# Even and odd tokens of the split activations stored in two halves and read alternately by the matmuls

## The chip, the core and the metric

The kernel runs on one core of one Trainium2 chip. The metric is the device time in microseconds (us) of one execution, as the median of several runs; lower is better. Five units of the core appear below: TensorE (PE for its matmuls, PEld for loading the stationary operand), VectorE (DVE), ScalarE (ACT), GpSimd (POOL) and SyncE (SP, which here only starts transfers).

## What is computed

Two layers of a decoder trunk on 256 tokens with 16 learned meta tokens ahead of them (272 in all), model width 2048, hidden width 8192, all in float32:

```python
h = concat(meta, x)                                       # 272 tokens x 2048
h = h + gla_mixer(rmsnorm(h), w_in, ..., w_out)           # layer 0: gated linear attention
h = h + (relu(rmsnorm(h) @ w_up) ** 2) @ w_down           # layer 0: MLP
k_sh, v_sh = split(rmsnorm(h) @ w_kv)                     # shared keys and values
h = h + swa_mixer(rmsnorm(h), k_sh, v_sh, w_q, sinks, w_out)   # layer 1: windowed attention
h = h + (relu(rmsnorm(h) @ w_up) ** 2) @ w_down           # layer 1: MLP
return rmsnorm(h[16:])
```

Nearly all of the arithmetic is in the projections: activations of 272 tokens (256 in layer 1, where the meta tokens are needed no more) times weight matrices that are read from HBM once.

## The kernel before

The stream `h` stays in SBUF transposed: 16 tiles of 128 features (partitions) by 272 tokens. A projection is cut into output tiles of 128 features. For each one, `product` fetches two halves of 128x1024 weights (SP starts the transfer), splits each into a rounded part and a rest, and lets TensorE add up 16 steps of 128 input features in one PSUM bank. The weights are the stationary operand (128x128), the activations the moving one, one column for each token.

Every float32 operand is held as two float32r numbers, `hi` (rounded) and `lo` (the rest), and a product is `hi*hi + hi*lo + lo*hi`. For weights `split_weight` makes the two (a ScalarE copy on L89, a VectorE subtraction on L91). For activations the class `Split` (L94) wraps one tile of `2n` columns, `hi` in columns 0 to n and `lo` in columns n to 2n. Such tiles are made in five places:

- `split_x` (L152 to L155): ScalarE scales a stream tile into `x.hi` (L154), VectorE makes `x.lo` (L155); 80 times, for each projection that reads the stream.
- the gated outputs `y` of the linear attention (L691, L692): 16 times.
- the hidden tiles `hid` of the MLP (L720, L721): 128 times.
- the attention outputs `O`, one tile of 16 x 2 x 256 columns that is written from PSUM in pieces: eight of 2 x 240 tokens (L884, L885) and two small ones for the last 16 tokens of each head.

The matmuls that read them are in `passes` (L101). With n = 256 it is "wide": one matmul streams `hi` and `lo` together, 512 columns, into the two halves of a PSUM bank (L109), and a second one adds the weights' rest times `hi`, 256 columns (L110). With n = 272 (layer 0), or where `apart` is false (the query projection, the first round of the attention's output projection, the last product), three matmuls go to one place (L112, L113, L114). The first stage, in which the stream arrives in pieces, issues the same three kinds of matmul by hand (`passes_of` on L273, `block` on L280 and L282, and `rank` on L267).

```python
nc.tensor.matmul(ps[:, :2 * n], wh, x.both, start=begin, stop=False)       # L109
nc.tensor.matmul(ps[:, n:2 * n], wl, x.hi, start=False, stop=end)          # L110
```

The order of TensorE's work is fixed: in the first stage and in the windowed attention by hand-written schedules, elsewhere by the order of the program, which a planner lays out by its own estimate of times. ScalarE and VectorE split weights ahead of TensorE (three buffers each of `hi` and `lo`, four of raw weights), and between these they finish the products.

Of the kernel before, what the change touches and what calls it, by code (L numbers as in the profile page):

```python
# [12 lines left out]
F32R = mybir.dt.float32r  # L13
# [6 lines left out]
P = 128  # L20
D = 2048
KT = D // P
HK = KT // 2
NM = 16
SEQ = 256
L = NM + SEQ
# [19 lines left out]
GRP = QH // KVH  # L46
# [18 lines left out]
def trunk(ctx: ExitStack, tc: tile.TileContext, a: dict, out: bass.AP):  # L65
    nc = tc.nc
# [19 lines left out]
    def split_weight(raw):  # L86
# [4 lines left out]
        nc.vector.tensor_sub(lo, raw, hi.bitcast(F32))  # L91
        return hi, lo

    class Split:  # L94


        def __init__(self, tile_, n):
            self.n, self.both = n, tile_[:, :2 * n]
            self.hi, self.lo = self.both[:, :n], self.both[:, n:]

    def passes(ps, hi, lo, xs, first, last, m=P, apart=True):  # L101

        n = xs[0].n
        wide = apart and 2 * n <= 512
        for k, x in enumerate(xs):
            wh, wl = hi[:, k * m:(k + 1) * m], lo[:, k * m:(k + 1) * m]
            begin, end = first and k == 0, last and k == len(xs) - 1
            if wide:
                nc.tensor.matmul(ps[:, :2 * n], wh, x.both, start=begin, stop=False)  # L109
                nc.tensor.matmul(ps[:, n:2 * n], wl, x.hi, start=False, stop=end)  # L110
            else:
                nc.tensor.matmul(ps[:, :n], wh, x.hi, start=begin, stop=False)  # L112
                nc.tensor.matmul(ps[:, :n], wh, x.lo, start=False, stop=False)  # L113
                nc.tensor.matmul(ps[:, :n], wl, x.hi, start=False, stop=end)  # L114

    def product(src, xs, raws=None, halves=(0, 1), after=None, apart=True, begun=None, pool=acc):

# [33 lines left out]

    def split_x(src, scale_col):  # L152
        x = Split(xp.tile([P, 2 * L], F32R, tag="x", name="x"), src.shape[-1])
        nc.scalar.activation(x.hi, src, AF.Copy, scale=scale_col)  # L154
        nc.vector.scalar_tensor_tensor(x.lo, src, scale_col, x.hi.bitcast(F32), ALU.mult, ALU.subtract)  # L155
        return x
# [59 lines left out]
    with ExitStack() as gla:  # L216
# [35 lines left out]
        wrs = bp.tile([P, KT, RG * 32], F32R, tag="Q", name="wrs")  # L252
        nc.gpsimd.memset(wrs.bitcast(F32), 0.0)
        groups = wrs.rearrange("p k (g r) -> p k g r", r=32)
        xs, sq = [], Square()
        ps_r = aux.tile([P, 512], F32, tag="aux", name="ps_r")
# [5 lines left out]
        def rank(k0, k1):  # L262

            for k in range(k0, k1):
                parts = [(RG * 32, xs[k].hi), ((RG - 1) * 32, xs[k].lo)]
                for i, (m, part) in enumerate(parts if k < KT - 1 else parts[::-1]):
                    nc.tensor.matmul(ps_r[:m, :L], wrs[:, k, :m], part, start=k + i == 0, stop=k + i == KT)  # L267

        first = [(acc if m < 4 else aux).tile([P, 512], F32, tag="acc" if m < 4 else "aux", name="ps") for m in range(NF)]

        def passes_of(m, k, t, w, j):

            nc.tensor.matmul(first[m][:, :L], w[t // 2][:, j * P:(j + 1) * P], xs[k].lo if t == 1 else xs[k].hi, start=k + t == 0, stop=False)  # L273

        def block(m, k0, k1, w):

            for part in range(2):
                for k in range(k0, k1):
                    wk = w[part][:, (k - k0) * P:(k - k0 + 1) * P]
                    nc.tensor.matmul(first[m][:, :L], wk, xs[k].hi, start=False, stop=part == 1 and k == KT - 1)  # L280
                    if part == 0:
                        nc.tensor.matmul(first[m][:, :L], wk, xs[k].lo, start=False, stop=False)  # L282

        def room():
            return [wp.tile([P, HK * P], F32R, tag=t, name=t) for t in ("hi", "lo")]
# [28 lines left out]
        with tc.manual_schedule(engines={mybir.EngineType.PE, mybir.EngineType.Activation, mybir.EngineType.DVE}):  # L314
# [3 lines left out]
            for u in range(2):  # L318
                for m in range(NF):
                    if m == u == 0:  # L320
                        take(0, 1)
                    if m % 2 == 0:
                        w = room()
                    part = m % 2
# [12 lines left out]
            for i, raw in enumerate(pairs):  # L337
                w = room()
                m0, m1 = max(2 * i - 1, 0), 2 * i + 1
# [7 lines left out]
            w = second(0)  # L347
# [4 lines left out]
            w = second(1)  # L352
# [3 lines left out]
            w = second(2)  # L356
# [3 lines left out]
            w = second(3)  # L360
# [27 lines left out]
        with tc.issue_after(scaled_keys.ins):  # L388
            for m in range(NF, 8):
                ps, = product(a["w_in"][8 + m], xs, begun=w5 if m == NF else None, pool=aux if m == NF else acc)  # L390
# [22 lines left out]
        for m in range(8):  # L413
            log_gate(m)
            ps, = product(a["w_in"][m], xs)
# [260 lines left out]
        for m in range(KT):  # L676
            g, mm = divmod(m, 4)
            if mm == 0:
                mix(g)
            ps, = product(a["w_in"][32 + m], xs)  # L680
            gt = tp.tile([P, L], F32, tag="t1", bufs=4, name="gt")
            nc.vector.tensor_mul(gt, ps, rs)
            sg = tp.tile([P, L], F32, tag="t2", bufs=4, name="sg")
            nc.gpsimd.tensor_scalar_max(sg, gt, -80.0)
            nc.scalar.activation(sg, sg, AF.Exp, scale=-1.0)
            nc.scalar.activation(sg, sg, AF.Ln, bias=1.0)
            nc.scalar.activation(sg, sg, AF.Exp, scale=-1.0)
            nc.vector.tensor_mul(gt, gt, sg)
            nc.vector.scalar_tensor_tensor(gt, OT[g][:, mm], no[:, mm:mm + 1], gt, ALU.mult, ALU.mult)
            y = Split(yp.tile([P, 2 * L], F32R, tag="y", bufs=KT, name="y"), L)  # L690
            nc.scalar.copy(y.hi, gt)  # L691
            nc.vector.tensor_sub(y.lo, gt, y.hi.bitcast(F32))  # L692
            ys.append(y)
# [11 lines left out]
    def mlp(layer, xs, sq, cols, finish):  # L705
        n = cols.stop - cols.start
        rs = sq.rstd(D, "rs", split=True)
        with tc.tile_pool(name="hid", bufs=KT) as hp, tc.tile_pool(name="wp2", bufs=1) as wp2:
            for b in range(NB):
                hs = []  # L710
                for m in range(KT):
                    if b == 0 and m == 4:
                        pools.append(wp2)
                    ps = total(product(a[f"w_up{layer}"][b * KT + m], xs))
                    u = tp.tile([P, L], F32, tag="t1", bufs=4, name="u")[:, :n]
                    nc.vector.scalar_tensor_tensor(u, ps, 0.0, rs, ALU.max, ALU.mult)
                    u2 = tp.tile([P, L], F32, tag="t2", bufs=4, name="u2")[:, :n]
                    nc.scalar.square(u2, u)
                    y = Split(hp.tile([P, 2 * L], F32R, tag="hid", name="hid"), n)
                    nc.scalar.copy(y.hi, u2)  # L720
                    nc.vector.tensor_sub(y.lo, u2, y.hi.bitcast(F32))  # L721
                    hs.append(y)
                for m in range(KT):
                    ending = layer == 1 and b == NB - 1 and m == KT - 1
                    for term in product(a[f"w_down{layer}"][b * KT + m], hs, apart=not ending):
                        nc.vector.tensor_add(h[m][:, cols], h[m][:, cols], term)
                    if b == NB - 1:
                        finish(m)
            pools.remove(wp2)
# [12 lines left out]
    with ExitStack() as swa:  # L742
# [62 lines left out]
                nc.scalar.copy(VT[i][:n, g], pt[:n, i * P:(i + 1) * P])  # L805


        O = ap.tile([P, KT, 2, SEQ], F32R, name="O")
        N1, N3 = P - NM, NM
        N2 = N1 + P  # L810

# [24 lines left out]
        class Step:  # L836
# [39 lines left out]
            def values(self):  # L876
                PT, m0 = self.PT, self.m0
                ps = acc.tile([P, 512], F32, tag="acc", name="ps_pv")
                pv = ps[:, :2 * N2].rearrange("p (i q) -> p i q", i=2)
                for t, q, begin, end in ((0, slice(0, N1), True, True), (1, slice(N1, N2), True, False), (2, slice(N1, N2), False, True)):  # L880
                    for par, kv in enumerate(HALVES):
                        nc.tensor.matmul(pv[kv, :, q], VT[t // 2][:, self.pair, kv], PT[t][:, 2 * par:2 * par + 2, :q.stop - q.start], start=begin, stop=end)  # L882
                oh, ol = O[:, m0:m0 + 2, 0, :N2], O[:, m0:m0 + 2, 1, :N2]
                nc.scalar.copy(oh, pv)  # L884
                nc.vector.tensor_sub(ol, pv, oh.bitcast(F32))  # L885

# [22 lines left out]
            def last_values(self):  # L909
                ps = aux.tile([P, 512], F32, tag="aux", name="ps_pv3")  # L910
                for b, nb in enumerate((P, P, NM)):
                    for t, kv in zip(self.PT3, HALVES):
                        nc.tensor.matmul(ps[kv, :P], VT[b][:nb, self.pair, kv], t[:nb, b], start=(b == 0), stop=(b == 2))
                ms = slice(self.pair * GRP, (self.pair + 1) * GRP)
                src = ps[:, :P].rearrange("p (i q) -> p i q", q=N3)
                oh, ol = O[:, ms, 0, N2:], O[:, ms, 1, N2:]
                nc.scalar.copy(oh, src)
                nc.vector.tensor_sub(ol, src, oh.bitcast(F32))

# [7 lines left out]
        with tc.manual_schedule(engines={mybir.EngineType.PE}):  # L927
            steps = []
            for t in range(2 * GRP // 2):
# [23 lines left out]
                for i in range(2):  # L953
# [3 lines left out]
            late = {3: [a4.values, partial(a6.scores, 0), partial(a6.scores, 1)], 5: [a5.transposes],  # L957
                    7: [a5.values, partial(a7.scores, 0), partial(a7.scores, 1)], 8: [a7.last_scores, a6.transposes],
                    10: [a6.values], 11: [a7.transposes], 12: [a7.last_transposes], 13: [a7.values, a7.last_values]}
            ys = [Split(O[:, m].rearrange("p a n -> p (a n)"), SEQ) for m in range(KT)]  # L960
            residual(a["w_out_b"], ys, X, to_mlp, rounds=2, between=late)

    fin = ctx.enter_context(tc.tile_pool(name="fin", bufs=1))
# [95 lines left out]
```

## Time and profile before

| | |
|---|---|
| median of 3 runs | 2179.11 us (2179.04 to 2180.6) |
| span of the profiled execution, first to last instruction | 2177.8 us |
| PE busy / PEld busy | 2163.8 us (99%) / 2055.6 us (94%) |
| DVE / ACT / POOL busy | 1367.1 us (63%) / 1079.2 us (50%) / 194.9 us (9%) |
| moved by the DMA engines | 383.85 MB, 176 GB/s on the mean |
| mean granted TensorE clock | 0.998 |

The profile holds the span alone; the time of the same execution around it isn't given, and the median stands 1.3 us above the span. [...]

### The profile page before, as it was taken

How to read it: one execution, taken by the hardware profiler on the slowest of the kernel's cores; microseconds unless marked ns; L12 is line 12 of the kernel's file. 1: busy time of each engine (PE TensorE's matmuls, PEld its weight loads, DVE VectorE, ACT ScalarE, POOL GpSimd, SP SyncE). 2: the span in 40 equal slices, each digit the busy share in tenths (PEclk: the TensorE clock that was granted, in tenths of full speed). 3: DMA queues.
4: the chain of work that ended last, by engine and by line, in shares of the span. 5: the costliest groups of instructions: out<-in, count | busy, mean ns of one | idle time of the engine just before them, and what ended most of it. 6: DMA issues, size and time to landing. Idle time of an engine off the chain costs nothing.

```text
span 2177.8 us, 39097 instructions
## 1 busy us (share of the span) xinstructions
PE 2163.8 (99%) x15978; PEld 2055.6 (94%) x15978; DVE 1367.1 (63%) x1999; ACT 1079.2 (50%) x1729; POOL 194.9 (9%) x209
## 2 busy tenths in 40 slices
PE   9999999999999999999999999999999999999997
PEld 9999999999999999999999999988888888888886
DVE  7799667655455445545556767686656656666665
ACT  6556664444344334433444578755435535544543
POOL 0000123300000000000013111060000000000022
PEclk9999999999999999999999999999999999999999
DMA  7544445555555555555554654465555555555552
GB/s 234 178 153 139 144 148 184 178 210 175 175 174 175 176 176 176 176 174 177 176 175 136 196 167 150 135 229 187 191 187 192 187 191 187 191 187 190 190 187 97
DMA packets 109124, 383.85 MB, mean 176 GB/s; under 512 B 13328, under 2 KB 15888, under 8 KB 108944
## 3 DMA queue, kind: packets, MB, share of 16 engines
q1 hardware_dynamic: 106640, 378.29, 51.7%
q0 software_dynamic: 1152, 2.38, 0.4%
q8 instruction: 125, 2.05, 0.4%
q10 hardware_dynamic: 1152, 0.68, 0.1%
q14 instruction: 55, 0.45, 0.1%
HBM read 376.82 MB, written 2.10 MB: 174 GB/s over the span
## 4 chain that ended last, share of the span: by engine, by line
PE 99%; DMA 0%; DVE 0%; SPq 0%; ACT 0%; issue 0%; DVEq 0%
PE ps L109 23%; PE ps L112 20%; PE ps L114 20%; PE ps L113 20%; PE ps L110 12%; PE ps L280 1%; PE s L860 1%; PE ps_pv L882 1%; PE pt L871 0%; PE ps L282 0%; PE ps_o L667 0%; DMA h<-in_h 0%; PE ps_l L542 0%; DVE scaled L979 0%; PE ps_r L267 0%; DMA raw<-in_w_in 0%
## 5 line engine op out<-in xcount | busy, mean ns | idle before, releaser
L91 DVE TENSOR_TENSOR lo<-raw,hi 128x1024 fp32r<-128x1024 f32 x707 | 872.6, 1235 | 577.7 <-ACT hi L89 570.6
L89 ACT CAST hi<-raw 128x1024 fp32r<-128x1024 f32 x707 | 741.1, 1049 | 991.8 <-PE ps L113 546.5
L112 PE MATMUL ps<-x,hi 128*128 128x272 f32 (+1 forms) x2032 | 585.8, 288 | 0.0
L114 PE MATMUL ps<-x,lo 128*128 128x272 f32 (+1 forms) x2032 | 585.0, 288 | 0.0
L113 PE MATMUL ps<-x,hi 128*128 128x272 f32 (+1 forms) x2032 | 584.5, 288 | 0.0
L113 PEld LDWEIGHTS ps<-x,hi 128*128 128x128 f32 x2032 | 386.0, 190 | 0.3 <-DVE x L155 0.2
L112 PEld LDWEIGHTS ps<-x,hi 128*128 128x128 f32 x2032 | 382.5, 188 | 2.5 <-issue 2.3
L114 PEld LDWEIGHTS ps<-x,lo 128*128 128x128 f32 x2032 | 381.6, 188 | 0.3
L109 PE MATMUL ps<-x,hi 128*128 128x512 f32 x1024 | 357.0, 392 | 0.0
L109 PE MATMUL ps<-hid,hi 128*128 128x512 f32 x1008 | 351.0, 392 | 0.0
L114 PE MATMUL ps<-hid,lo 128*128 128x272 f32 (+1 forms) x1040 | 299.9, 288 | 0.0
L112 PE MATMUL ps<-hid,hi 128*128 128x272 f32 (+1 forms) x1040 | 299.9, 288 | 0.0
L113 PE MATMUL ps<-hid,hi 128*128 128x272 f32 (+1 forms) x1040 | 299.4, 288 | 0.0
L110 PE MATMUL ps<-x,lo 128*128 128x256 f32 x1024 | 287.7, 281 | 0.0
L110 PE MATMUL ps<-hid,lo 128*128 128x256 f32 x1008 | 282.6, 281 | 0.0
L109 PEld LDWEIGHTS ps<-x,hi 128*128 128x128 f32 x1024 | 192.0, 188 | 42.9
L109 PEld LDWEIGHTS ps<-hid,hi 128*128 128x128 f32 x1008 | 188.8, 188 | 41.9
L113 PEld LDWEIGHTS ps<-hid,hi 128*128 128x128 f32 x1040 | 197.8, 190 | 0.0
L112 PEld LDWEIGHTS ps<-hid,hi 128*128 128x128 f32 x1040 | 195.4, 188 | 0.0
L114 PEld LDWEIGHTS ps<-hid,lo 128*128 128x128 f32 x1040 | 195.4, 188 | 0.0
L110 PEld LDWEIGHTS ps<-x,lo 128*128 128x128 f32 x1024 | 193.2, 189 | 0.0
L110 PEld LDWEIGHTS ps<-hid,lo 128*128 128x128 f32 x1008 | 190.2, 189 | 0.3
(259 smaller groups left out, 2102.6 us busy)
## 6 DMA issues: line engine op xcount, KB each, us to landing
raw<-in_w_up SPq DMA_DIRECT2D x256, 512.0 KB, 3.3
raw<-in_w_down SPq DMA_DIRECT2D x256, 512.0 KB, 3.3
raw<-in_w_in SPq DMA_DIRECT2D x91, 512.0 KB, 3.3
raw<-in_w_out_a SPq DMA_DIRECT2D x32, 512.0 KB, 3.3
raw<-in_w_q SPq DMA_DIRECT2D x32, 512.0 KB, 3.5
raw<-in_w_out_b SPq DMA_DIRECT2D x32, 512.0 KB, 3.3
raw<-in_w_kv SPq DMA_DIRECT2D x8, 512.0 KB, 3.4
sw<-qt POOLq DMA_DIRECT2D x32, 64.0 KB, 3.8
```

What stands on the lines that cost most here:

```text
L89: nc.scalar.copy(hi, raw)
L91: nc.vector.tensor_sub(lo, raw, hi.bitcast(F32))
L109: nc.tensor.matmul(ps[:, :2 * n], wh, x.both, start=begin, stop=False)
L110: nc.tensor.matmul(ps[:, n:2 * n], wl, x.hi, start=False, stop=end)
L112: nc.tensor.matmul(ps[:, :n], wh, x.hi, start=begin, stop=False)
L113: nc.tensor.matmul(ps[:, :n], wh, x.lo, start=False, stop=False)
L114: nc.tensor.matmul(ps[:, :n], wl, x.hi, start=False, stop=end)
L280: nc.tensor.matmul(first[m][:, :L], wk, xs[k].hi, start=False, stop=part == 1 and k == KT - 1)
L860: nc.tensor.matmul(s[:, i * n:(i + 1) * n], self.QR[pp, i, o:o + P], KR[pp, self.pair, :n], start=True, stop=True)
L882: nc.tensor.matmul(pv[kv, :, q], VT[t // 2][:, self.pair, kv], PT[t][:, 2 * par:2 * par + 2, :q.stop - q.start], start=begin, stop=end)
```

## The change

`Split` keeps its size, but its `2n` columns are ordered anew: even tokens of `hi`, even tokens of `lo`, odd tokens of `hi`, odd tokens of `lo`, each n/2 columns. `hi` and `lo` become views with the token order restored: element 0 from the first half, element 1 from the second, element 2 from the first again, and so on, each step n columns (1088 bytes with n = 272, 1024 bytes with n = 256) forth and then back to the next column. Every matmul that streams an activation reads in this alternating order and writes PSUM in the same order of tokens as before. The instructions that make the split tiles read their inputs in the order of tokens and write, and in the second of each pair also read `hi`, alternately. `O` gets the same order. No instruction is added or removed, and no size of a matmul or of a tile changes.

```diff
         def __init__(self, tile_, n):
-            self.n, self.both = n, tile_[:, :2 * n]
-            self.hi, self.lo = self.both[:, :n], self.both[:, n:]
+            self.n, self.both = n, tile_[:, :2 * n].rearrange("p (a s j) -> p s j a", a=2, s=2)
+            self.hi, self.lo = self.both[:, 0], self.both[:, 1]
...
+    def pairs_of(t):
+
+        return t.rearrange("p (j a) -> p j a", a=2)
...
             if wide:
-                nc.tensor.matmul(ps[:, :2 * n], wh, x.both, start=begin, stop=False)
-                nc.tensor.matmul(ps[:, n:2 * n], wl, x.hi, start=False, stop=end)
+                both = ps[:, :2 * n].rearrange("p (s j a) -> p s j a", s=2, a=2)
+                nc.tensor.matmul(both, wh, x.both, start=begin, stop=False)
+                nc.tensor.matmul(both[:, 1], wl, x.hi, start=False, stop=end)
             else:
-                nc.tensor.matmul(ps[:, :n], wh, x.hi, start=begin, stop=False)
-                nc.tensor.matmul(ps[:, :n], wh, x.lo, start=False, stop=False)
-                nc.tensor.matmul(ps[:, :n], wl, x.hi, start=False, stop=end)
+                out = pairs_of(ps[:, :n])
+                nc.tensor.matmul(out, wh, x.hi, start=begin, stop=False)
+                nc.tensor.matmul(out, wh, x.lo, start=False, stop=False)
+                nc.tensor.matmul(out, wl, x.hi, start=False, stop=end)
...
     def split_x(src, scale_col):
         x = Split(xp.tile([P, 2 * L], F32R, tag="x", name="x"), src.shape[-1])
+        src = pairs_of(src)
         nc.scalar.activation(x.hi, src, AF.Copy, scale=scale_col)
         nc.vector.scalar_tensor_tensor(x.lo, src, scale_col, x.hi.bitcast(F32), ALU.mult, ALU.subtract)
...
-        O = ap.tile([P, KT, 2, SEQ], F32R, name="O")
+        O = ap.tile([P, KT, 2, 2, SEQ // 2], F32R, name="O")
+
+        def attended(part, ms, tokens):
+
+            return O[:, ms, :, part, tokens.start // 2:tokens.stop // 2].rearrange("p m a j -> p m j a")
```

The rest of the diff does the same to the first stage's matmuls (L267, L273, L280, L282), to `y` (L691), `hid` (L720) and the two places that write `O` (L884, L917).

More of the change, by code (lines that the diff above doesn't have):

```diff
@@ L266, in rank @@
                 for i, (m, part) in enumerate(parts if k < KT - 1 else parts[::-1]):
-                    nc.tensor.matmul(ps_r[:m, :L], wrs[:, k, :m], part, start=k + i == 0, stop=k + i == KT)
+                    nc.tensor.matmul(pairs_of(ps_r[:m, :L]), wrs[:, k, :m], part, start=k + i == 0, stop=k + i == KT)
         first = [(acc if m < 4 else aux).tile([P, 512], F32, tag="acc" if m < 4 else "aux", name="ps") for m in range(NF)]
         def passes_of(m, k, t, w, j):
-            nc.tensor.matmul(first[m][:, :L], w[t // 2][:, j * P:(j + 1) * P], xs[k].lo if t == 1 else xs[k].hi, start=k + t == 0, stop=False)
+            nc.tensor.matmul(pairs_of(first[m][:, :L]), w[t // 2][:, j * P:(j + 1) * P], xs[k].lo if t == 1 else xs[k].hi, start=k + t == 0, stop=False)
         def block(m, k0, k1, w):
@@ L279, in block @@
                     wk = w[part][:, (k - k0) * P:(k - k0 + 1) * P]
-                    nc.tensor.matmul(first[m][:, :L], wk, xs[k].hi, start=False, stop=part == 1 and k == KT - 1)
+                    out = pairs_of(first[m][:, :L])
+                    nc.tensor.matmul(out, wk, xs[k].hi, start=False, stop=part == 1 and k == KT - 1)
                     if part == 0:
-                        nc.tensor.matmul(first[m][:, :L], wk, xs[k].lo, start=False, stop=False)
+                        nc.tensor.matmul(out, wk, xs[k].lo, start=False, stop=False)
         def room():
@@ L690, in trunk @@
             y = Split(yp.tile([P, 2 * L], F32R, tag="y", bufs=KT, name="y"), L)
+            gt = pairs_of(gt)
             nc.scalar.copy(y.hi, gt)
@@ L719, in mlp @@
                     y = Split(hp.tile([P, 2 * L], F32R, tag="hid", name="hid"), n)
+                    u2 = pairs_of(u2)
                     nc.scalar.copy(y.hi, u2)
@@ L882, in values @@
                         nc.tensor.matmul(pv[kv, :, q], VT[t // 2][:, self.pair, kv], PT[t][:, 2 * par:2 * par + 2, :q.stop - q.start], start=begin, stop=end)
-                oh, ol = O[:, m0:m0 + 2, 0, :N2], O[:, m0:m0 + 2, 1, :N2]
+                oh, ol = (attended(part, slice(m0, m0 + 2), slice(0, N2)) for part in range(2))
+                pv = pv.rearrange("p i (j a) -> p i j a", a=2)
                 nc.scalar.copy(oh, pv)
@@ L914, in last_values @@
                 ms = slice(self.pair * GRP, (self.pair + 1) * GRP)
-                src = ps[:, :P].rearrange("p (i q) -> p i q", q=N3)
-                oh, ol = O[:, ms, 0, N2:], O[:, ms, 1, N2:]
+                src = ps[:, :P].rearrange("p (i j a) -> p i j a", i=GRP, a=2)
+                oh, ol = (attended(part, ms, slice(N2, SEQ)) for part in range(2))
                 nc.scalar.copy(oh, src)
@@ L959, in trunk @@
                     10: [a6.values], 11: [a7.transposes], 12: [a7.last_transposes], 13: [a7.values, a7.last_values]}
-            ys = [Split(O[:, m].rearrange("p a n -> p (a n)"), SEQ) for m in range(KT)]
+            ys = [Split(O[:, m].rearrange("p a s j -> p (a s j)"), SEQ) for m in range(KT)]
             residual(a["w_out_b"], ys, X, to_mlp, rounds=2, between=late)
```

## Prediction, made before the changed kernel ran

> **What bounds the kernel now.** I read first the page's busy times, then the chain of waits that ended last.
>
> ```profile
> PE 2163.8 (99%) x15978; PEld 2055.6 (94%) x15978; DVE 1367.1 (63%) x1999; ACT 1079.2 (50%) x1729; POOL 194.9 (9%) x209
> ...
> PEclk9999999999999999999999999999999999999999
> ...
> PE 99%; DMA 0%; DVE 0%; SPq 0%; ACT 0%; issue 0%; DVEq 0%
> PE ps L109 23%; PE ps L112 20%; PE ps L114 20%; PE ps L113 20%; PE ps L110 12%; PE ps L280 1%; PE s L860 1%; PE ps_pv L882 1%; PE pt L871 0%; PE ps L282 0%; PE ps_o L667 0%; DMA h<-in_h 0%; PE ps_l L542 0%; DVE scaled L979 0%; PE ps_r L267 0%; DMA raw<-in_w_in 0%
> ```
>
> TensorE works from end to end at full clock, and 95% of the chain are the five matmul lines that stream split activations: the very operands that the change lays out anew. VectorE has 2177.8 - 1367.1 = 811 us to spare, ScalarE 1099 us. So the question is what one column of those matmuls costs. Busy times overlap; I take the timeline of TensorE, starts in the first column.
>
> ```profile
> 999.96 0.28 PE L112 MATMUL ps<-hid,hi 128*128 128x272 f32 x1
> ...
> 1016.91 0.29 PE L112 MATMUL ps<-x,hi 128*128 128x272 f32 x1
> ```
>
> Between these lie 135 matmuls of 272 columns: 16.95 us / 135 = 125.6 ns from start to start.
>
> ```profile
> 1263.07 0.28 PE L114 MATMUL ps<-x,lo 128*128 128x256 f32 x1
> ...
> 1272.70 0.28 PE L114 MATMUL ps<-x,lo 128*128 128x256 f32 x1
> ```
>
> 81 matmuls of 256 columns: 9.63 / 81 = 118.9 ns. Sixteen columns more cost 6.7 ns, 0.42 ns each, and 118.9 - 256 x 0.42 = 11.4 ns belong to each matmul whatever its length.
>
> ```profile
> 1499.88 0.39 PE L109 MATMUL ps<-x,hi 128*128 128x512 f32 x1
> ...
> 1519.73 0.39 PE L109 MATMUL ps<-x,hi 128*128 128x512 f32 x1
> ```
>
> 57 pairs of 512 and 256 columns: 348.2 ns; less 118.9, the wide one takes 229.3 ns, 0.43 ns for each column beyond 256. I use 0.42.
>
> **The change, part by part.** *The streams of TensorE.* How many columns are read in the new order comes from the groups by line, shapes kept apart.
>
> ```profile
> L112 PE MATMUL ps<-x,hi 128*128 128x272 f32 x1776 | 512.9, 289 | 0.0
> ...
> L109 PE MATMUL ps<-x,hi 128*128 128x512 f32 x1024 | 357.0, 392 | 0.0
> L109 PE MATMUL ps<-hid,hi 128*128 128x512 f32 x1008 | 351.0, 392 | 0.0
> L112 PE MATMUL ps<-hid,hi 128*128 128x272 f32 x1024 | 295.4, 288 | 0.0
> ...
> L112 PE MATMUL ps<-y,hi 128*128 128x272 f32 x256 | 73.5, 288 | 0.0
> ...
> L112 PE MATMUL ps<-x,hi 128*128 128x256 f32 x256 | 72.9, 285 | 0.0
> ...
> L109 PE MATMUL ps<-O,hi 128*128 128x512 f32 x128 | 44.4, 390 | 0.0
> L112 PE MATMUL ps<-O,hi 128*128 128x256 f32 x128 | 36.6, 286 | 0.0
> ```
>
> L113 and L114 repeat each L112, L110 follows each L109. So 3 x (1776 + 1024 + 256) = 9,168 matmuls of 272 columns; 3 x (256 + 128 + 16) = 1,200 of 256, the 16 being the last product; 2,160 pairs of 768; and, by the loops of the code, 272 of 272 columns in the first stage. That is 14,960 matmuls and 2,493,696 + 307,200 + 1,658,880 + 73,984 = 4,533,760 columns, 1,904 us at 0.42 ns: seven eighths of the span is the reading of these columns, one after another out of adjacent addresses. After the change no two successive columns are adjacent; each lies about a kilobyte from the one before.
>
> No matmul of the trace reads its moving operand so, so its price must be bounded by other engines' rows. Two VectorE reductions sum over elements that lie 64 bytes apart (`ident` and `am5`, read every 16th column):
>
> ```profile
> L452 DVE TENSOR_REDUCE fold<-ident 80x16 f32<-80x80 f32 x1 | 0.3, 292 | 0.0
> L431 DVE TENSOR_REDUCE block<-ident 128x64 f32<-128x128 f32 x1 | 0.3, 256 | 0.0
> L639 DVE TENSOR_REDUCE am<-am 80x32 f32<-80x160 f32 x2 | 0.9, 434 | 0.0
> L522 DVE TENSOR_TENSOR E<-B 128x1024 f32<-128x1024 f32 x12 | 14.6, 1217 | 0.0
> L530 DVE TENSOR_TENSOR W<-E,Q 128x256 f32<-128x256 f32 x24 | 9.0, 417 | 0.0
> ```
>
> From 80 to 160 such elements takes 434 - 292 = 142 ns more, 1.775 ns each, while an element costs (1217 - 417) / 768 = 1.042 ns on the two ordinary rows: 1.70 times, or 0.73 ns lost for each jump. Short runs alone aren't the cause: L431 sums 64 pairs of adjacent elements and takes 256 ns for 128, less than 80 jumping ones. ScalarE shows a milder case, the exponentials of L524 and L525 on halves of 4, then 2, then single alternate elements:
>
> ```profile
> 186.93 0.62 ACT L524 ACTIVATE E<-E 128x512 f32<-128x512 f32 x1
> 187.44 0.63 ACT L525 ACTIVATE E<-E 128x512 f32<-128x512 f32 x1
> ...
> 192.83 0.68 ACT L524 ACTIVATE E<-E 128x512 f32<-128x512 f32 x1
> 193.40 0.68 ACT L525 ACTIVATE E<-E 128x512 f32<-128x512 f32 x1
> ...
> 195.10 0.69 ACT L524 ACTIVATE E<-E 128x512 f32<-128x512 f32 x1 [0.55 <-DVE E L522]
> 195.68 0.67 ACT L525 ACTIVATE E<-E 128x512 f32<-128x512 f32 x1
> ```
>
> Where every 16 bytes still give two elements, 512 of them cost 0.055 us more, 0.107 ns each. So leaving adjacent addresses costs both engines time, and the more the fewer neighbours are used.
>
> For TensorE this gives: at the least nothing (a read ahead deep enough for two runs at once); VectorE's ratio, 0.70 x 1,904 = +1,333 us; VectorE's loss in ns, 0.73 x 4.534 million = +3,310 us. I take one lost column for every column, +1,904 us: the case nearest to ours is VectorE's (every element jumps), and TensorE, which moves on by whole columns, can't lose 0.70 of one each time. A gain isn't excluded either (below).
>
> [...]
>
> *The instructions that write the tiles.* No instruction is added. The rows give what is written alternately on VectorE; ScalarE has the same counts.
>
> ```profile
> L155 DVE SCALAR_TENSOR_TENSOR x<-h,gains,x 128x272 fp32r<-128x272 f32 x48 | 38.6, 819 | 5.6 <-ACT x L154 5.6
> L721 DVE TENSOR_TENSOR hid<-u,hid 128x272 fp32r<-128x272 f32 x64 | 27.7, 433 | 0.0
> L721 DVE TENSOR_TENSOR hid<-u,hid 128x256 fp32r<-128x256 f32 x64 | 26.8, 419 | 0.0
> ```
>
> With 32 more `x` of 256, 16 `y` and the pieces of `O` that is some 63,000 elements an engine; at nothing to 0.73 ns each, up to 46 us on either (92 on VectorE if its read and write add up), about 0.2 us an instruction. It hides behind TensorE: the two have 811 and 1,099 us idle, and the last hidden tile of a block is wanted only by the last step of the next product, 45 matmuls (5.7 us) after its first, against some 1.8 us from product to tile. Without that cover, at the start, 16 tiles of `x` would add at most 16 x 0.2 = 3 us. The transfers, the weight splits and PSUM's order stay; a slower TensorE asks for weights later, so nothing else is late.
>
> *Sum.* 2177.8 + 1,904 = 4,082 us of span, 1.3 us more by the median: 4,083 us. Its own bounds: 2,179 + 1,333 = 3,512 and 2,179 + 3,310 = 5,489.
>
> **The rivals.** *Two runs open at once (chance 0.17).* If TensorE's reading keeps both places ready, a column stays at 0.42 ns and only the writers change: 2,179 us, up to 2,182 with the first stage's 3 us. For it: the pattern is two plain runs, not a wide scatter as in L639. Against it: ScalarE lost time even where neighbours lie 8 bytes apart.
>
> A row for the next one, a plain exponential on ScalarE:
>
> ```profile
> L562 ACT ACTIVATE QE<-B 128x1024 f32<-128x1024 f32 x2 | 2.1, 1060 | 0.5 <-DVE W L530 0.5
> ```
>
> *The jump has a fixed price in time (0.12).* If 1.775 ns is what any engine waits for a new place, whatever its own pace, TensorE goes from 0.42 to 1.775 ns: + 1.355 x 4.534 million = 6,143 us, 8,322 us. For it: ScalarE's two elements at (0.85 + 0.107) ns, 0.85 being (1060 - 625) / 512 from this row and the first two of L524 and L525, make 1.91 ns for 16 bytes, close to 1.775. Against it: TensorE takes 16 bytes in 4 x 0.42 = 1.68 ns now and shows no such floor.
>
> *Faster: two places feed the stream better than one (0.06).* The 11.4 ns for each matmul are spent outside its columns. If they are the start of a read that waits for its first place, and two places in turn hide it, 14,960 matmuls x 11.4 ns = 171 us go: 2,008 us. It decides from the point where 256 columns start less than 118.9 ns apart; the smallest sign would be 1 ns each, 15 us. Against it: the gap doesn't grow with the columns (272 and 256 agree), so it isn't a matter of how they are read.
>
> *A part of it (0.12).* If only some jumps cost, as on ScalarE (0.107 of 0.85 ns, 13%, for each element), a column costs 0.47 ns: + 240 us, 2,420 us, and anything up to 3,500.
>
> **How the numbers follow.** The forecast has 0.53, with 3,512 to 5,489 us of its own; the likeliest time is 4,083 us. The range must reach down to the rival without effect and the partial one: 2,170 to 5,500 us holds 0.53 + 0.17 + 0.12, and leaves out the fixed price and the gain, 0.18. Two times of this kernel within 0.2% (4.4 us) can't be told apart. Faster: 0.06. Same: of the first rival's 0.17, 0.14, as its 3 us may come with more waiting. Slower: the rest, 0.80.
>
> **What would show it.** In the changed kernel's timeline three-pass matmuls of 272 columns start 2 x 272 x 0.42 + 11.4 = 240 ns apart, those of 256 columns 226 ns, a wide pair 668 ns; TensorE stays at 99% and the busy share of VectorE falls to about a third. The step is wrong if the starts stay at 125.6 ns (first rival), go to 494 ns (fixed price) or fall under 125 ns (the gain). The writers' step is right if L721's kind takes 433 to 630 ns and the chain names TensorE alone; it is wrong if the chain shows waits for `hid` or `x` in the middle of the run.

## The result, and the profile after

The changed kernel takes 2062.5 us (median of 4 runs, 2060.31 to 2063.95) against 2179.09 us of the kernel before beside it (2179.04 to 2180.6): a ratio of 0.9462, 95% interval 0.9449 to 0.9475. It is 117 us faster, where 1,904 us more were forecast. Its profiled execution took 2060.31 us.

The profile's page of the changed kernel: span, busy times with their counts, and granted clock.

```profile
span 2058.6 us, 39099 instructions
...
PE 2030.5 (99%) x15978; PEld 1951.3 (95%) x15978; DVE 1404.8 (68%) x1999; ACT 1130.7 (55%) x1729; POOL 202.3 (10%) x209
...
PEclk9999999999999999999999999999999999999999
```

The counts are those of before, and TensorE is still busy for 99% of the span; VectorE and ScalarE work 38 and 52 us longer. So the same matmuls took less time each. The timeline of TensorE, starts in the first column, shows it; L118 to L120 are the three passes (before: L112 to L114), L114 and L115 the wide pair (before: L109 and L110).

```profile
1000.12 0.28 PE L118 MATMUL ps<-x,hi 128*128 128x272 f32 x1
...
1019.93 0.28 PE L118 MATMUL ps<-x,hi 128*128 128x272 f32 x1
...
1171.63 0.28 PE L118 MATMUL ps<-x,hi 128*128 128x256 f32 x1
...
1184.02 0.28 PE L118 MATMUL ps<-x,hi 128*128 128x256 f32 x1
...
1400.12 0.38 PE L114 MATMUL ps<-x,hi 128*128 128x512 f32 x1
...
1431.88 0.38 PE L114 MATMUL ps<-x,hi 128*128 128x512 f32 x1
```

Between the first two lie 171 matmuls of 272 columns, 19.81 / 171 = 115.8 ns each (before 125.6); between the next two 111 of 256 columns, 111.6 ns (118.9); between the last two 97 pairs, 327.4 ns (348.2). Times the prediction's counts that is 9,440 x 9.8 + 1,200 x 7.3 + 2,160 x 20.8 ns = 92.5 + 8.8 + 44.9 = 146 us. Adding up the distances from each of these 14,960 matmuls to the next start, where one of over 150 ns (250 for a wide matmul) is put at the mean of its line, gives 2,078.3 us before and 1,934.9 after, 143.4 less, while the span fell by 119.2. The other 24 us were given back: 13.1 as stretches in which the start behind a split matmul came late, 11.0 around the other matmuls (the norms' sums and the two attention stages).

Not all of these 24 us are waits. The clock's row above shows means of some 51 us; inside it two stretches of 3.4 us, from 279.6 and from 1228.5 us, had a granted clock of 0.51, and the 15 split matmuls of the first one stand 227 ns apart. Nearly all matmuls from 6.3 to 9.8 us stand so too, though the profile gives a clock of 1.00 there. At half the pace the three stretches, 10.3 us together, lose up to 5 us, an estimate. The kernel before had no stretch of lower clock until its last 8 us (0.51).

Where TensorE waits is in its view of waits, total, count and longest in us; first the longest of the changed kernel, then one of the kernel before.

```profile
PE ps_ssq L190 <- ACT sqh L188: 3.7, 2, 1.9
PE ps_l L550 <- DVE W L538: 2.6, 3, 1.5
PE ps L119 <- DVE x L162: 2.3, 2, 1.3
```

```profile
PE ps L280 <- ACT hi L291: 1.1, 1, 1.1
```

Before, this was one of only two waits of a microsecond or more, both in the first 15 us; now several results of ScalarE and VectorE come a microsecond or two late, and the rows of the view add up to 16.9 us against 2.9. The instructions that write the tiles are among what they do, and they got slower (groups by line, shapes kept apart; L730 and L731 were L720 and L721):

```profile
L730 ACT CAST hid<-u 128x272 fp32r<-128x272 f32 x64 | 43.8, 685 | 2.0
L731 DVE TENSOR_TENSOR hid<-u,hid 128x272 fp32r<-128x272 f32 x64 | 40.2, 630 | 0.0
```

and of the kernel before, for ScalarE, whose row the prediction doesn't show:

```profile
L720 ACT CAST hid<-u 128x272 fp32r<-128x272 f32 x64 | 26.9, 421 | 2.0
```

L731 takes 630 ns against L721's 433: 197 ns for 272 elements, 0.72 ns each. L730 takes 685 ns against 421, 0.97 ns each.

### The profile page after: what moved, and what is told of

Its sections match the earlier page's. It is cut to its first block, busy times and chain, and to the rows that moved or that the text cites. A ratio compares the mean times of both kernels' runs of the same rounds, so it can differ in the third digit from the quotient of the medians.

```text
span 2058.6 us, 39099 instructions
## 1 busy us (share of the span) xinstructions
PE 2030.5 (99%) x15978; PEld 1951.3 (95%) x15978; DVE 1404.8 (68%) x1999; ACT 1130.7 (55%) x1729; POOL 202.3 (10%) x209
## 5 line engine op out<-in xcount | busy, mean ns | idle before, releaser
L119 PE MATMUL ps<-x,hi 128*128 128x272 f32 (+1 forms) x2032 | 567.4, 279 | 2.3 <-DVE x L162 2.3
L118 PE MATMUL ps<-x,hi 128*128 128x272 f32 (+1 forms) x2032 | 568.6, 280 | 0.0
L120 PE MATMUL ps<-x,lo 128*128 128x272 f32 (+1 forms) x2032 | 567.6, 280 | 0.3 <-DVE lo L91 0.3
L118 PEld LDWEIGHTS ps<-x,hi 128*128 128x128 f32 x2032 | 385.5, 190 | 2.6 <-issue 2.1
L120 PEld LDWEIGHTS ps<-x,lo 128*128 128x128 f32 x2032 | 385.3, 190 | 1.1 <-DVE lo L91 0.6
L114 PE MATMUL ps<-x,hi 128*128 128x512 f32 x1024 | 335.9, 382 | 0.0
L114 PE MATMUL ps<-hid,hi 128*128 128x512 f32 x1008 | 330.1, 382 | 0.0
L118 PE MATMUL ps<-hid,hi 128*128 128x272 f32 (+1 forms) x1040 | 290.1, 279 | 0.0
L119 PE MATMUL ps<-hid,hi 128*128 128x272 f32 (+1 forms) x1040 | 290.1, 279 | 0.0
L120 PE MATMUL ps<-hid,lo 128*128 128x272 f32 (+1 forms) x1040 | 290.1, 279 | 0.0
L115 PE MATMUL ps<-x,lo 128*128 128x256 f32 x1024 | 279.2, 273 | 0.0
L115 PE MATMUL ps<-hid,lo 128*128 128x256 f32 x1008 | 274.1, 273 | 0.0
L114 PEld LDWEIGHTS ps<-x,hi 128*128 128x128 f32 x1024 | 193.5, 189 | 27.0 <-DVE x L162 0.2
L114 PEld LDWEIGHTS ps<-hid,hi 128*128 128x128 f32 x1008 | 190.2, 189 | 26.4
L115 PEld LDWEIGHTS ps<-x,lo 128*128 128x128 f32 x1024 | 196.6, 192 | 0.3 <-DVE lo L91 0.3
L118 PEld LDWEIGHTS ps<-hid,hi 128*128 128x128 f32 x1040 | 196.6, 189 | 0.0
L120 PEld LDWEIGHTS ps<-hid,lo 128*128 128x128 f32 x1040 | 196.6, 189 | 0.0
L115 PEld LDWEIGHTS ps<-hid,lo 128*128 128x128 f32 x1008 | 193.5, 192 | 0.2
```

What stands on the lines that cost most here:

```text
L114: nc.tensor.matmul(both, wh, x.both, start=begin, stop=False)
L115: nc.tensor.matmul(both[:, 1], wl, x.hi, start=False, stop=end)
L118: nc.tensor.matmul(out, wh, x.hi, start=begin, stop=False)
L119: nc.tensor.matmul(out, wh, x.lo, start=False, stop=False)
L120: nc.tensor.matmul(out, wl, x.hi, start=False, stop=end)
```

## The experiments

### Which part of the change makes the matmuls faster

`e1_streams` is the kernel before with 35 series of 64 equal matmuls behind its last product; each series has its own line, so its matmuls' distance is the start of the next series less its own start, by 64. All operands are float32r, the output goes to one PSUM bank. Work is only added, so the whole time tells nothing.

```diff
+    for i in range(64): nc.tensor.matmul(ps[:, :272], W[i % 8], T[:, :272], ...)           # contiguous, L1006
+    for i in range(64): nc.tensor.matmul(pairs(ps[:, :272]), W[i % 8], alt(T, 272, 272), ...)  # alternate, L1007
...
+    # and others: runs of 2, 4, 8; every 2nd, 4th, 8th column; other distances, lengths, weights
```

> The kernel before, with 35 series of 64 matmuls behind its last product, each on a source line of its own, all on one split-type tile T of 2304 columns and one tile W of weights (sets of 128 in turn), 272 columns unless the series says otherwise; only the first two series after the warm-up run beside copies on ScalarE and subtractions on VectorE, then those engines are idle. The series add nothing to the output and some 270 us to the time. Read is the distance from start to start. In the projections it was 125.6 ns contiguous and 115.9 ns alternate. Theory A, the two reads of TensorE collide (the weights of the next matmul are loaded while the columns of this one stream): contiguous stays near 125 with the other engines idle; with 32 weights instead of 128 it falls by about three quarters of the 10 ns, to 118 or less, and alternate stays near 116. Theory B, the streams collide with ScalarE's and VectorE's traffic: contiguous is 125 beside the copies and 116 without them. Theory C, a pattern of two dimensions is read ahead in another way: two runs with a gap take 116 like alternate. Theory D, adjacent columns (the same 16 bytes) cost and a jump frees them: runs of 4 and of 8 and two runs with a gap stay near 125, runs of 2 lie between, every 4th and every 8th column take 116. Theory E, a distance does it: near 4 and near 8 stay at 125, only the far half takes 116.

The timeline of TensorE: L1002 contiguous and L1003 alternate, while ScalarE copies and VectorE subtracts; VectorE goes on until 2222.6 us, so that L1006 and L1007 still run beside it, and from L1009 on nothing else runs. L1006 contiguous, L1007 alternate from halves 272 columns apart, L1008 two runs with a gap between, L1009 two halves in runs of two columns; L1012 alternating within each eight columns (0, 4, 1, 5, ...); L1014 every second column.

```profile
2175.05 8.19 PE L1002 MATMUL ps_b<-T,W 128*128 128x272 f32 x64
2183.08 7.58 PE L1003 MATMUL ps_b<-T,W 128*128 128x272 f32 x64
2190.49 8.19 PE L1004 MATMUL ps_b<-T,W 128*128 128x272 f32 x64
...
2206.55 8.18 PE L1006 MATMUL ps_b<-T,W 128*128 128x272 f32 x64
2214.56 7.57 PE L1007 MATMUL ps_b<-T,W 128*128 128x272 f32 x64
2221.97 8.26 PE L1008 MATMUL ps_b<-T,W 128*128 128x272 f32 x64
2230.07 11.42 PE L1009 MATMUL ps_b<-T,W 128*128 128x272 f32 x64
2241.32 8.49 PE L1010 MATMUL ps_b<-T,W 128*128 128x272 f32 x64
...
2257.97 7.58 PE L1012 MATMUL ps_b<-T,W 128*128 128x272 f32 x64
2265.38 7.58 PE L1013 MATMUL ps_b<-T,W 128*128 128x272 f32 x64
2272.79 15.74 PE L1014 MATMUL ps_b<-T,W 128*128 128x272 f32 x64
2288.35 15.96 PE L1015 MATMUL ps_b<-T,W 128*128 128x272 f32 x64
```

The kernel's two distances stand here in series of their own: contiguous (2214.56 - 2206.55) / 64 = 125.2 ns, alternate 115.8. Beside both other engines they are 125.5 and 115.8, with both idle 125.3 and 115.8 (L1004 and L1005 of the next run), and in two later series with a quarter of the weight columns 124.4 and 115.9: neither the traffic of others nor the number of weights to load makes the difference. How the weights lie can still show: where they are read every second column, alternate takes 119.8 ns and contiguous 124.5. A pattern of two contiguous runs (126.6) gains nothing, so it isn't the form of the pattern. Nor is the distance what counts: halves 16 bytes apart (L1012, 115.8 ns) do as well as 1,088. And the order can hurt badly: runs of two 175.8, every second column 243.1 ns (every fourth, L1015, 246.6). All five theories of the expectation fall.

### What counts as a neighbour

What was left is a rule F, the author's guess from these series: float32r columns are read as two streams, the even ones and the odd ones, and each stream does well while it stays within the 16 bytes that it read last. By it, contiguous reading uses each 16 bytes twice in either stream, alternate reading four times, every second column once.

```diff
+    ... alt within blocks of four columns, and of eight shifted by 8 bytes             # L1006, L1008
+    ... alternate, and in each half only every 2nd / every 4th column                  # L1009, L1010
+    ... the same from bf16 tiles: contiguous, alternate, every 2nd, every 4th column   # L1017 to L1020
```

> The kernel before, with 26 series of 64 matmuls of 272 columns behind its last product, each on its own source line; nothing is added to the output. Theory F, formed on the first series: TensorE reads its moving columns as two streams, the even columns and the odd ones, and each stream keeps the 16 bytes it read last; four successive hits of a stream on the same 16 bytes run at 116 ns a matmul, two at 125, one at about 240. Theory G: what counts is only that a pattern's innermost dimension is two columns that aren't adjacent. Float32r series: contiguous 125 by both; alternate 272 and near 4 (columns 0, 4, 1, 5, ...) 116 by both; near 2 (0, 2, 1, 3, 4, 6, ...) 125 by F, 116 by G; near 4 shifted by 8 bytes 125 by F, 116 by G; alternate with every 2nd column of each half 125 by F, 116 by G; alternate with every 4th 240 by F, 116 by G; every 3rd and every 5th 240 by both; four and eight columns in turn from as many runs 175 to 240 by F (116 by a rule that any jump helps); one pair of columns again and again 116 by F. Bfloat16, eight columns in 16 bytes, by F: contiguous 116 (four hits a stream), so alternate gains nothing; every 2nd 125, every 4th and 8th 240, alternate with every 2nd 116, with every 4th 125. By G, or if the 16 bytes don't matter, contiguous bfloat16 is 125 and alternate 116, every 2nd 240 as with float32r. Plain float32 is in as a look, without a number.

The same view, with the other engines idle; L1004 is contiguous and L1005 alternate from halves 272 columns apart, L1007 is the alternation within eight columns again, L1008 the same 8 bytes on.

```profile
2183.10 8.18 PE L1004 MATMUL ps_b<-T,W 128*128 128x272 f32 x64
2191.12 7.58 PE L1005 MATMUL ps_b<-T,W 128*128 128x272 f32 x64
2198.53 8.27 PE L1006 MATMUL ps_b<-T,W 128*128 128x272 f32 x64
2206.64 7.58 PE L1007 MATMUL ps_b<-T,W 128*128 128x272 f32 x64
2214.05 8.12 PE L1008 MATMUL ps_b<-T,W 128*128 128x272 f32 x64
2222.01 7.84 PE L1009 MATMUL ps_b<-T,W 128*128 128x272 f32 x64
2229.70 15.66 PE L1010 MATMUL ps_b<-T,W 128*128 128x272 f32 x64
2245.18 15.83 PE L1011 MATMUL ps_b<-T,W 128*128 128x272 f32 x64
...
2319.38 7.59 PE L1017 MATMUL ps_b<-T,W 128*128 128x272 bf16 x64
2326.80 16.71 PE L1018 MATMUL ps_b<-T,W 128*128 128x272 bf16 x64
2343.35 7.89 PE L1019 MATMUL ps_b<-T,W 128*128 128x272 bf16 x64
```

Where F and G part, float32r went with F: four uses of the 16 bytes by one stream, 115.8 ns (L1007); two, 126.7 (L1006), 124.4 (L1008) and 120.2 (L1009, which lies between F's 125 and G's 116); one, 241.9 (L1010). The shift by 8 bytes alone costs 8.6 ns, as a boundary of 16 bytes would have it; contiguous runs that begin 2, 4 or 16 columns later (`e1_streams`: 126.6, 124.4, 126.6) stay within 2.2 ns of each other. It did not carry over to bf16, where F expected about 116 for the alternate order: contiguous takes 115.9, alternate 258.6, every second column 120.8, every fourth 241 (L1020). Plain float32 lost by alternating too, 36.9 us for a series against 31.2, although the granted clock was 1.00 for the first and 0.94 for the second. F missed float32r orders as well. In runs of two and in four places in turn no 16 bytes are used twice in succession by one stream, which is about 240 ns by F; they take 176.0 and 146.8 ns, the second outside the 175 to 240 that were expected. One pair of columns again and again takes 119.1 ns where F has 116.

### Is it paid by the matmul or by the column

`e5_lengths` varies the length, contiguous and alternate, takes the two in turn, and reads bf16 in runs.

```diff
+    ... n = 128, 192, 256, 320, 384, 448, 512: contiguous, then alternate                  # L1004 to L1017
+    ... 272 columns, contiguous and alternate in turn                                      # L1018
+    ... bf16 from two halves in runs of 2, 4 and 8                                         # L1019 to L1021
```

> The kernel before with 23 more series of 64 matmuls behind its last product; the time tells nothing, the pitch (start to start) inside each series does. 'contiguous' reads n columns in one run, 'alternate' reads the same n columns from two halves in turn, for n = 128, 192, 256, 320, 384, 448, 512. Theory S (what contiguous reading loses is a start of every read that has no slack to be caught up): the difference contiguous minus alternate is about the same at every length, 8 to 12 ns, and both grow by 0.41 to 0.42 ns a column. Theory R (contiguous reading runs at a slightly lower rate in every column): the difference grows with the length, from about 4 ns at 128 columns to 12 ns at 512. A series that takes contiguous and alternate matmuls in turn (272 columns): by both theories the mean pitch is the mean of the two, about 120.6 ns; if a contiguous matmul loses only behind another contiguous one, it is 116. bf16, where the alternate order took 258.6 ns against 116.0 for one run: in runs of 2, 4 and 8 columns from two halves, by theory L (bf16 is one stream that keeps one 16-byte line, every change of place costs one more line) the pitch falls with the length of the run, to about 240, 180 and 116 ns; by a fixed cost of the two-dimensional order it stays near 259. bf16 with 512 columns in one run against every second column: 216 and about 220 if that loss is a start, 216 and about 225 if it goes by the column.

```profile
2183.28 7.26 PE L1004 MATMUL ps_b<-T,W 128*128 128x128 f32 x64
2190.38 7.30 PE L1005 MATMUL ps_b<-T,W 128*128 128x128 f32 x64
...
2219.54 7.31 PE L1009 MATMUL ps_b<-T,W 128*128 128x256 f32 x64
2226.69 9.55 PE L1010 MATMUL ps_b<-T,W 128*128 128x320 f32 x64
2236.08 8.86 PE L1011 MATMUL ps_b<-T,W 128*128 128x320 f32 x64
2244.77 11.26 PE L1012 MATMUL ps_b<-T,W 128*128 128x384 f32 x64
2255.87 10.56 PE L1013 MATMUL ps_b<-T,W 128*128 128x384 f32 x64
2266.27 13.14 PE L1014 MATMUL ps_b<-T,W 128*128 128x448 f32 x64
2279.25 12.27 PE L1015 MATMUL ps_b<-T,W 128*128 128x448 f32 x64
2291.35 14.71 PE L1016 MATMUL ps_b<-T,W 128*128 128x512 f32 x64
2305.90 13.98 PE L1017 MATMUL ps_b<-T,W 128*128 128x512 f32 x64
2319.71 7.87 PE L1018 MATMUL ps_b<-T,W 128*128 128x272 f32 x64
2327.42 9.45 PE L1019 MATMUL ps_b<-T,W 128*128 128x272 bf16 x64
```

At 320 columns contiguous takes 146.7 and alternate 135.8 ns, at 512 columns 227.3 and 215.8: 10.9 and 11.5 ns apart. From 320 to 512 the alternate order grows by 80.0 / 192 = 0.417 ns a column, which leaves 2.4 ns for the matmul; contiguous by 0.420, which leaves 12.4. At 384 columns the two are 10.9 ns apart again (173.4 and 162.5), at 272 they were 9.4, where theory R has about 7. So theory S fits better: the price of contiguous reading is some 10 ns for every matmul and changes little with its length. It doesn't fit everywhere, for 448 columns (202.8 and 189.1) are 13.7 ns apart, which neither theory has. Alternate float32r and contiguous bf16 agree at 272 columns (115.8 and 115.9 ns); contiguous float32r, with 125.2, stands apart.

Below 256 columns there is nothing to win: 128 and 192 columns take 111 to 112 ns in either order (L1004 to L1007, of which the first pair is shown), and 256 columns alternate 111.7, the same floor. Alternate reading at 256 would otherwise come to 256 x 0.417 + 2.4 = 109.2 ns, so the floor takes 2.5 ns of the gain there. The kernel's wide pairs don't show this floor: in the changed kernel the matmul behind one of 256 columns (L115) starts 109.3 ns after it, the mean of 2,160. The mixed series (L1018) has 120.5 ns, the mean of the two; by the starts of its single records the next matmul follows a contiguous one after 125.0 ns and an alternate one after 115.7, so each pays for its own order. For bf16 the distance falls with the length of the run: alternate 258.6, runs of two 145, of four 120, of eight 115.8 ns (L1019 to L1021, the last by its single records). The direction is theory L's and so is its 116 for the last; its 240 and 180 aren't. And bf16's loss by reading every second column goes by the column: about 5 ns at 272 columns, 10 at 512 (226 against 216 by the single records).

### Only the writers, and the writers without their price

`e4_writers` has the changed kernel's tiles and its writers, and lets every matmul read each half as one run. PSUM then holds the tokens in another order than the rest of the program takes them to be, so that the output isn't the reference's; the amount of work is the same.

```diff
-                out = pairs_of(ps[:, :n])
-                nc.tensor.matmul(out, wh, x.hi, start=begin, stop=False)
+                out = runs_of(ps[:, :n])        # p (a j) -> p a j
+                nc.tensor.matmul(out, wh, x.rhi, start=begin, stop=False)
```

> The changed kernel's tiles and writers, but the matmuls read each half as one run (even tokens, then odd tokens), so that PSUM and with it everything behind holds the tokens in another order than the rest of the program takes them to be: the output is not the reference's, the work is the same. Theory F gives 126.5 ns a matmul as in the series of two runs with a gap, some 15 us over before's 125.5, plus what the slower writers cost TensorE in waits: 2,205 to 2,220 us if that is the 20 us that are missing from the gain, 2,190 to 2,197 if the writers are hidden. If the gain came from the way the tiles are written or where they lie, and not from the order of reading, this kernel would be at 2,060.

`e3_halves` turns it round: the tiles keep the order of before, `hi` then `lo`, and are written in one run; the matmuls read the first and the second half of the tokens alternately. PSUM then holds token 0, n/2, 1, n/2 + 1 and so on, and whoever reads PSUM takes every second column.

```diff
-            self.n, self.both = n, tile_[:, :2 * n].rearrange("p (a s j) -> p s j a", a=2, s=2)
-            self.hi, self.lo = self.both[:, 0], self.both[:, 1]
+            self.n, both = n, tile_[:, :2 * n]
+            self.hi, self.lo = both[:, :n], both[:, n:]
+            self.both = both.rearrange("p (s a j) -> p s j a", s=2, a=2)
+            self.rhi, self.rlo = self.both[:, 0], self.both[:, 1]
...
-        return [ps[:, t * n:(t + 1) * n] for t in range(2 if apart and 2 * n <= 512 else 1)]
+        return [in_order(ps[:, t * n:(t + 1) * n]) for t in range(2 if apart and 2 * n <= 512 else 1)]
...
-                    nc.vector.scalar_tensor_tensor(u, ps, 0.0, rs, ALU.max, ALU.mult)
+                    nc.vector.scalar_tensor_tensor(by_halves(u), ps, 0.0, by_halves(rs), ALU.max, ALU.mult)
```

> The tiles lie in order again, hi then lo, and are written as before; every matmul reads the two halves of hi and of lo alternately (token 0, token n/2, token 1, ...), and PSUM holds the tokens in that shuffled order; the VectorE and ScalarE instructions that read a product put them back by reading PSUM every second column. If the whole gain is the order in which TensorE reads (9,440 matmuls of 272 columns by 9.7 ns, 1,200 of 256 by 7 ns, 2,160 pairs by 20 ns: 143 us) and the alternating writers gave some 20 us of it back, then the writers are at 420 to 435 ns again, TensorE's waits fall back to before's 14 us, and the time is 2,037 to 2,048 us. If the shortfall comes from something else (a faster TensorE outruns the weight splits), it stays at 2,060. If reading PSUM every second column costs VectorE what jumps cost it in SBUF, the time is 2,060 or more.

The profile's page and the timeline, first of `e4_writers`:

```profile
PE 2157.5 (99%) x15978; PEld 2048.1 (94%) x15978; DVE 1411.4 (65%) x1999; ACT 1138.3 (52%) x1729; POOL 194.9 (9%) x209
...
1000.01 0.29 PE L124 MATMUL ps<-hid,hi 128*128 128x272 f32 x1
...
1019.80 0.29 PE L124 MATMUL ps<-x,hi 128*128 128x272 f32 x1
```

and the same of `e3_halves`, with the groups of the hidden tiles' `lo` and of the first reader of PSUM in the MLP:

```profile
PE 2024.2 (99%) x15978; PEld 1946.3 (95%) x15978; DVE 1362.9 (67%) x1999; ACT 1074.8 (52%) x1729; POOL 194.8 (10%) x209
...
1000.15 0.28 PE L128 MATMUL ps<-x,hi 128*128 128x272 f32 x1
...
1019.95 0.28 PE L128 MATMUL ps<-x,hi 128*128 128x272 f32 x1
...
L737 DVE TENSOR_TENSOR hid<-u,hid 128x272 fp32r<-128x272 f32 x64 | 27.7, 434 | 0.0
L732 DVE SCALAR_TENSOR_TENSOR u<-ps,rstd 128x272 f32<-128x272 f32 x64 | 28.3, 442 | 37.0 <-PE ps L130 37.0
```

`e4_writers`: 2177.78 us, ratio 0.9994 (0.9984 to 1.0003), no difference that can be told, and less than either range of its expectation. Its 159 matmuls lie 124.5 ns apart, where 126.5 was expected and before has 125.6, and VectorE and ScalarE carry about the same longer busy times as in the changed kernel (the hidden tiles' `lo` takes 650 ns). Added up as above, the split matmuls come to 2,070.8 us, 7.5 less than before, and 4.2 us are given back by late starts and around the other matmuls. So the 117 us are not the layout's, and at TensorE's old pace the slower writers cost 4 us at most; why these runs are read 1.1 ns faster than before's stays open.

`e3_halves`: 2050.39 us (2049.86 to 2051.62), ratio 0.9409 (0.9393 to 0.9425), somewhat over its expectation, and faster than both kernels. Its 171 matmuls lie 115.8 ns apart as in the changed kernel, while L737 is back at 434 ns. Taking every second column of PSUM costs these readers nothing: L732 has 442 ns, and had 442 (L716) where it read PSUM in one run; L742 has 438 as L726 had, and ScalarE's copy on L152 366 where L136 had 367. It is 12.1 us faster than the changed kernel by the medians and 9.6 by the spans (2058.6 - 2049.0), where up to 5 of the 9.6 are the three stretches with 227 ns a matmul or a clock of 0.51, which this trace doesn't have. So the slower writers cost some 5 to 12 us once TensorE runs faster. The other 14.6 us of the 24 given back remain in it. Its view of waits adds up to 13.3 us, 10.4 more than before's (the longest again on L550's kind, 2.6 us in three): there the faster TensorE now overtakes results that used to be ready in time. That is read from the waits alone; no run took one of them away.

## Why the prediction was wrong

**What bounds the kernel: right.** TensorE from end to end (busy 99% of the span before and after), by those five lines; it was its pace that moved the time. The counts were right too.

**The price of a column on TensorE: wrong, and it is the step that failed.** "I take one lost column for every column, +1,904 us: the case nearest to ours is VectorE's (every element jumps)." VectorE's rows were of one stepping run, 64 bytes a step. TensorE does pay about the column that was forecast for such a run: every second column takes (243.1 - 125.2) / 272 = 0.43 ns more a column, and the 240 ns that were forecast for the alternate order are there to be seen on L1014. But two runs in turn are not a stepping run to it: the order gains 10 ns a matmul in place of losing 114. Rule F would explain it by even and odd columns keeping their places apart, each walking through adjacent columns; it fits most of the float32r series by their times, and no run shows more of it. The rows of other engines could not show that, and the number taken from them was a whole column where the truth was below zero. That TensorE moves on by whole columns and can't lose a part of one was the author's estimate, which no run shows: in runs of two it lost (175.8 - 125.2) / 272 = 0.19 ns a column, less than half of one. Nor does the number of successive reads from the same 16 bytes set the price: every second column has two and takes 243.1 ns, the alternate order has none and takes 115.8. For bf16, where alternating takes 258.6 ns against 115.9, the forecast's direction would have been right, and its size too small by a fifth.

**The rival that came true was held at 0.06.** "Faster" put the 11.4 ns for each matmul down to the start of a read, and 2,008 us. It is the rival that fits the runs: the price is mainly by the matmul (10.9 ns at 320 columns, 11.5 at 512), and two places take it away; that it is the wait of a read for its first place no run shows. "The gap doesn't grow with the columns (272 and 256 agree), so it isn't a matter of how they are read" was the faulty argument against it; a price that doesn't grow with the columns can still depend on their order. Its size was off by two terms: some 1.8 of the 11.4 ns stay (143.4 us came, 9.6 ns a matmul, and not 171 us), and 24 us were given back, most of it in waits. 2179.1 - 143.4 + 24.2 = 2,059.9 us, against 2,060.31 of the profiled execution and 2,062.5 in the median.

**Two runs open at once** (no effect on the stream, 2,179 to 2,182 us) fails at the first sign given: starts stayed neither at 125.6 ns nor above. **The fixed price** and **a part of it** fail with the main step.

**The writers: the size right, the cover only at the old pace.** L731 takes 630 ns, the upper bound given; ScalarE's L730 loses 0.97 ns an element, which is over the bound of 0.73. They were said to hide behind TensorE. `e4_writers` shows that they do at 125 ns a matmul, but for 4 us at most, and `e3_halves` that they cost some 5 to 12 us at 116. "The chain shows waits for `hid` or `x` in the middle of the run" was the sign against it: in the view of waits those for `x` on L162 are there, 2.3 us in two at 1157 and 1159 us, of which 1.3 us stay in `e3_halves` with its fast writers; there is none for `hid`.

## What to carry to other kernels

When TensorE sets the end and its moving operands are float32r, compare its start-to-start distance with columns x 0.417 ns, the alternate order's pace from 320 to 512 columns in `e5_lengths`: here 12 to 16 ns over that, with contiguous tiles of 272 to 512 columns, were 9 to 14 ns of reading order, and reading two halves in turn gave them back. Keep the tiles contiguous for their writers and unshuffle where PSUM is read (2050.4 against 2062.5 us); don't do it for bf16 or plain float32, where the same order cost time (258.6 ns a matmul against 115.9, 36.9 us a series against 31.2). And don't price one engine's access pattern by another engine's rows: a series of 64 matmuls settles it.

## What the runs showed of the hardware that was not expected

- Contiguous reading is not the fastest order for float32r: 125.2 ns for 272 columns, 115.8 when two places are read in turn, even only 16 bytes apart.
- Most float32r orders in `e1_streams` and `e2_hits` follow how often the even columns by themselves, and the odd ones, use their 16 bytes: four times 115.8 ns, twice 120 to 127, once 240 to 247 (every eighth column 231). For bf16 it is not so: alternate columns 258.6 ns, contiguous 115.9.
- In the series of equal matmuls with 128 columns of weights no mean distance fell below 110 ns, down to 128 float32r columns (110.9 ns, L1004 of `e5_lengths`).
- Open: why two uses of 16 bytes cost a price mainly by the matmul and not by the column; no run shows the cause. Open too are runs of two (176 ns), of four and eight (130 ns), four places in turn (147 ns), and the 13.7 ns at 448 columns.
